# Where a mixture-of-experts kernel issues its loads of gates and activations, and how it splits expert weights

## The chip, the cores and the metric

The kernel runs on one core of one Trainium2 chip. The metric is the device time of one launch in microseconds (us). "Time before" is the median of three launches; the profile is of one further execution.

## The reference

Two transformer blocks over 512 tokens of width 1024, in float32. The first has attention and gated linear attention and then a PEER layer: 128 x 128 = 16384 experts, of which each token picks 16 in each of 8 heads. The second has pooling, spatial gating, a convolutional feed-forward layer and a gate at the end. The change lies in the PEER layer:

```python
q = (xi @ w_q).reshape(n, PEER_HEADS, 2, PEER_KEY_DIM)
...
gate = jax.nn.softmax(best_s, axis=-1)
act = jax.nn.gelu(jnp.einsum('nd,nhkd->nhk', xi, u[idx]), approximate=False)
return jnp.einsum('nhk,nhkd->nd', (gate * act).astype(xi.dtype), v[idx])
```

## The kernel before, in words

**Split operands.** Every large product is made with three matmuls (`mm3`, L86): an operand x is held as a high part (`whi` for weights), which ScalarE (ACT) writes by a rounding copy (L73), and a low part (`wlo`), which VectorE (DVE) writes as x minus the high part (L74). TensorE (PE) adds high times high, high times low and low times high. A weight block comes as one load into `wraw` from SyncE's queue (SP, L58), one block ahead in the program's order; eight `wraw` buffers exist in the expert stages (`c.more` is 5 there and 0 elsewhere). `split` (L64) works in two halves: for each half one tile of `whi` and one of `wlo`, four buffers of each, so two blocks.

**The PEER layer, dense.** For 384 of the 512 tokens all 16384 experts are computed, 128 to a block: an "up" block multiplies the tokens with `u` (24 matmuls of 384 columns) and ACT's Gelu empties the bank (L749); there are two banks. A "down" block multiplies gate times activation (`wh`, `wl`) with `v` into six accumulators (18 matmuls of 512 columns, L1064). The other 128 tokens go by gathered rows: GpSimd (POOL) fetches a row of `u` or `v` (L761), DVE multiplies it (L774) or adds it to an accumulator (L782).

**The two stages.** From about 480 to 965 us come the queries, the routing, and up blocks 0 to 95; the activations go to DRAM as `Ad`, the dense gates as `Gd`. The down stage (`down`, L1000, about 965 to 1640 us) goes through an order written by `down_order`: eight fresh up blocks, whose activations stay on chip (`fresh`), then three runs of eight stored down blocks, then the eight fresh ones as down blocks; and so on. Down blocks are weighed in groups of four: `weigh` (L1025) multiplies activations (`at`) by gates (`gt`) into `wt` on DVE (L1029), ACT copies the high part `wh` (L186), DVE makes the low part `wl` (L187). `gt` covers two groups, `at` one, two buffers each; `wt` has one buffer, `wh` and `wl` two.

**The loads in question.** `load` (L1015) issues `gt` (1.5 MB in runs of 512 bytes, 16 times) and `at` (768 KB, 24 times) from SP's queue, in the program's order eight steps before the group's first block; `weigh` stands two steps before it. `paced` makes a load wait for `c.step`, ACT's latest high-part copy. The gathers of rows are paced in the same way. The order of the instructions in each engine's queue is fixed when the program is built, from a modelled timeline (L1459), so an operation can stand earlier than its line suggests once the model has its inputs ready; on the chip each queue runs in that order.

Of the kernel before, what the change touches and what calls it, by code (L numbers as in the profile page):

```python
# [8 lines left out]
F32 = mybir.dt.float32  # L9
F32R = mybir.dt.float32r  # L10
# [5 lines left out]
ALU = mybir.AluOpType  # L16
# [4 lines left out]
P = 128  # L21
# [26 lines left out]
class Ctx:  # L48
# [15 lines left out]
    def split(self, raw, shape):  # L64

        nc = self.nc
        n = shape[0] // 2
        hi, lo = Halves(n), Halves(n)
        for i in range(2):
            x = raw[:, i * n:(i + 1) * n, :]  # L70
            for h, tag in ((hi, "whi"), (lo, "wlo")):
                h.append(self.wp.tile([P, n, shape[1]], F32R, tag=tag, name=tag, bufs=4))
            self.step = nc.scalar.copy(hi[i], x)  # L73
            nc.vector.tensor_tensor(lo[i], x, hi[i].bitcast(F32), ALU.subtract)  # L74
        return hi, lo

    def weights(self, jobs):
# [107 lines left out]
def split_plain(c, hi, lo, x):  # L185
    c.nc.scalar.copy(hi, x)  # L186
    c.nc.vector.tensor_tensor(lo, x, hi.bitcast(F32), ALU.subtract)  # L187
# [504 lines left out]
DT = ND * P  # L692
GT = 16
NG = DT // GT
JG = 4
JG2 = 2 * JG
NS = 96
KEEP = 1
LOAD = 8
WEIGH = 2  # L700
ROWS = 4
AFTER = 4
# [13 lines left out]
def peer_block(c):  # L716
# [4 lines left out]
    with ExitStack() as ctx:  # L721
# [78 lines left out]
        with ExitStack() as vctx:  # L800
            down(c, vctx, aux, up, bank)
# [198 lines left out]
def down(c, ctx, aux, up, bank):  # L1000
    nc, tc, I, X = c.nc, c.tc, c.I, c.X
    wk = ctx.enter_context(tc.tile_pool(name="pv", bufs=2))
    acc = [aux(f"acc{i}") for i in range(2 * ND)]
    acts, gts, ws = {}, {}, {}
    rate = (2 * P - c.n_rows) / (NKEYS + (NKEYS - NS) - 8)
    due = 0.0

    def turn():
        nonlocal due
        due += rate  # L1010
        while due >= 1:
            next(c.rows, None)
            due -= 1

    def load(j):  # L1015

        j0, b0 = j // JG2 * JG2, j % JG2
        if b0 == 0:
            gts[j0] = wk.tile([P, NG, JG2, GT], F32, name="gt")
            c.paced(nc.sync.dma_start(out=gts[j0], in_=c.Gd[:, :, j0:j0 + JG2, :].rearrange("n i j g -> i n j g")))  # L1020
        if j0 not in acts:
            ws[j] = wk.tile([P, JG, DT], F32, name="at")
            c.paced(nc.sync.dma_start(out=ws[j], in_=c.Ad[j // JG]))  # L1023

    def weigh(j):  # L1025
        j0, b0 = j // JG2 * JG2, j % JG2
        at = acts[j0][:, b0:b0 + JG, :] if j0 in acts else ws[j]
        wt = wk.tile([P, JG, NG, GT], F32, name="wt", bufs=1)
        nc.vector.tensor_tensor(wt, at.rearrange("p j (n g) -> p j n g", g=GT),  # L1029
                                gts[j0][:, :, b0:b0 + JG, :].rearrange("p n j g -> p j n g"), ALU.mult)  # L1030
        w = wt.rearrange("p j n g -> p j (n g)")
        ws[j] = [wk.tile([P, JG, DT], F32R, name=n) for n in ("wh", "wl")]
        split_plain(c, *ws[j], w)

    steps = [(what, j) for what, j0 in c.order for j in range(j0, j0 + JG2)]
    groups = [(s, j) for s, (what, j) in enumerate(steps) if what == "down" and j % JG == 0]
    to_load, to_weigh = list(groups), list(groups)
    n_done, batch = 0, []
    for s, (what, j) in enumerate(steps):
        while to_load and to_load[0][0] - s <= LOAD:  # L1040
            load(to_load.pop(0)[1])
        while to_weigh and to_weigh[0][0] - s <= WEIGH:
            weigh(to_weigh.pop(0)[1])
        if what == "up":
            if j % JG2 == 0:
                acts[j] = c.keep.tile([P, JG2, DT], F32, name="fresh")
            up(j, acts[j // JG2 * JG2][:, j % JG2, :])
            turn()
            continue
        wh, wl = ws[j // JG * JG]  # L1050
        vh, vl = next(c.peer_w)
        batch.append((j % JG, vh, vl))
        n_done += 1
        turn()
        if n_done == NKEYS - 1:
            continue

        last2 = n_done == NKEYS
        for hf in range(2):
            for t in range(ND):  # L1060
                tk = slice(t * P, (t + 1) * P)
                for bi, (jb, bh, bl) in enumerate(batch):
                    for pi, (x, y) in enumerate(((wh, bh), (wh, bl), (wl, bh))):
                        nc.tensor.matmul(acc[2 * t + hf], x[:, jb, tk], y.row(hf), start=n_done == 1 and pi == 0,  # L1064
                                         stop=last2 and bi == len(batch) - 1 and pi == 2)
        batch = []
    for _ in c.rows:
        pass
    for q in range(2):
        for t in (ND, *range(ND)):  # L1070
            if t < ND:
                y = wk.tile([P, 512], F32, tag=("at", "gt")[(q * ND + t) % 2], name="y")
                nc.scalar.copy(y, acc[2 * t + q])
            else:
                y = c.acc3[:, q * 512:(q + 1) * 512]
            o = bank("yt")
            for k in range(4):
                nc.tensor.transpose(o[:, k * P:(k + 1) * P], y[:, k * P:(k + 1) * P], c.ident)
            xs = X[:, 4 * q:4 * q + 4, t * P:(t + 1) * P]
            nc.vector.tensor_tensor(xs, xs, o.rearrange("p (k n) -> p k n", k=4), ALU.add)  # L1080
# [383 lines left out]
```

## Time and profile before

| what | us |
|---|---|
| median of 3 launches | 2466.18 |
| lowest and highest | 2461.13 and 2481.36 |
| the profiled execution, its own time | 2462.88 |
| its span, first to last instruction | 2461.1 |
| PE busy | 2401.9 |
| DVE busy | 1769.1 |
| ACT busy | 1200.6 |

The span is what the profile's rows divide up; 1.8 us of the execution's time lie outside it. PE, PEld, DVE, ACT and POOL are the engines (PEld is PE's loading of stationary operands, which runs beside the matmuls). "Busy" counts an instruction from its start to its end, with overlaps counted once; a matmul's end is modelled. The granted clock is the share of TensorE's full speed that the chip allowed in a stretch: 1.00 is 2.4 GHz, 0.50 is 1.2 GHz.

### The profile page before, as it was taken

What the parts mean: (1) busy time and instruction counts of PE and PEld (TensorE: products, weight loads), DVE (VectorE), ACT (ScalarE), POOL (GpSimd) and SP (SyncE); (2) the same over time, 40 slices, a digit from 0 to 9 for tenths busy, and PEclk for the clock granted to TensorE, in tenths of its full rate; (3) what the DMA queues carried; (4) which work ended last, traced back from release to release, by engine and by line L of the source; (5) the groups of instructions that cost most, each with busy time, mean ns of one, the idle gap of its engine ahead of it and who ended that gap; (6) DMA issues with size and microseconds to landing.
All of it is one profiled execution on the core that took longest, in us unless ns stands there. A gap on an engine that the chain in (4) does not pass through costs nothing.

```text
span 2461.1 us, 34465 instructions
## 1 busy us (share of the span) xinstructions
PE 2401.9 (98%) x12475; PEld 2095.1 (85%) x12475; DVE 1769.1 (72%) x3442; ACT 1200.6 (49%) x2163; POOL 380.6 (15%) x272
## 2 busy tenths in 40 slices
PE   8999899999999999999999999999999999999998
PEld 7888578999999999888878778779888888888888
DVE  5875769999899887786776776766764456777436
ACT  6334654446788995433333333335433335444335
POOL 0000000001333323333343432420000000000000
PEclk9999999999999999999999999999999999999999
DMA  4210034356999999988988888943232332232333
GB/s 138 69 52 27 26 117 143 101 183 209 324 359 349 334 332 359 359 308 287 351 274 301 319 286 307 323 169 100 86 99 95 97 100 96 95 98 97 94 105 103
DMA packets 170296, 471.80 MB, mean 192 GB/s; under 512 B 14060, under 2 KB 66157, under 8 KB 166798
## 3 DMA queue, kind: packets, MB, share of 16 engines
q1 hardware_dynamic: 133262, 335.37, 39.7%
q0 software_dynamic: 36864, 134.23, 15.7%
q8 instruction: 98, 1.61, 0.3%
q14 instruction: 72, 0.59, 0.1%
HBM read 421.31 MB, written 48.23 MB: 191 GB/s over the span
## 4 chain that ended last, share of the span: by engine, by line
PE 64%; DMA 8%; DVE 6%; issue 4%; POOL 1%; ACT 1%; SPq 0%; DVEq 0%; POOLq 0%; ACTq 0%
PE mm L97 51%; PE acc L1064 8%; PE G L946 3%; DMA row<-in_v_t_dram,ev 3%; DMA at<-Ad 2%; DVE wlo L74 2%; DMA wraw<-in_v_t_dram 1%; POOL row L761 1%; DVE acc L782 1%; DMA row<-in_peer_u_dram,eu 1%; PE sc L845 1%; DMA gt<-Gd 1%; DVE eq L898 0%; DVE ij L901 0%; SPq L1023 0%
## 5 line engine op out<-in xcount | busy, mean ns | idle before, releaser
L73 ACT CAST whi<-wraw 128x512 fp32r<-128x512 f32 (+3 forms) x902 | 547.6, 609 | 897.0 <-PE mm L97 524.6
L74 DVE TENSOR_TENSOR wlo<-wraw,whi 128x512 fp32r<-128x512 f32 (+3 forms) x902 | 595.4, 670 | 257.4 <-ACT whi L73 253.9
L97 PE MATMUL mm<-hi,whi 128*128 128x384 f32 (+3 forms) x2016 | 722.5, 363 | 19.8 <-ACT fresh L749 13.7
L97 PE MATMUL mm<-lo,whi 128*128 128x384 f32 (+3 forms) x2016 | 718.4, 361 | 0.5 <-DVE lo L182 0.4
L97 PE MATMUL mm<-hi,wlo 128*128 128x384 f32 (+3 forms) x2016 | 717.6, 361 | 0.3 <-DVE wlo L74 0.3
L97 PEld LDWEIGHTS mm<-hi,whi 128*128 128x128 f32 (+1 forms) x2016 | 377.4, 189 | 58.3 <-ACT fresh L749 14.7
L97 PEld LDWEIGHTS mm<-lo,whi 128*128 128x128 f32 (+1 forms) x2016 | 377.0, 189 | 38.2 <-DVE lo L182 1.7
L97 PEld LDWEIGHTS mm<-hi,wlo 128*128 128x128 f32 (+1 forms) x2016 | 376.9, 189 | 37.9 <-DVE wlo L74 1.9
L1064 PE MATMUL acc<-wlo,wh 128*128 128x512 f32 x768 | 300.8, 392 | 12.3 <-DVE wlo L74 12.3
L1064 PE MATMUL acc<-whi,wl 128*128 128x512 f32 x768 | 299.5, 390 | 0.0
L761 POOL DMA_INDIRECT row<-in_peer_u_dram,eu x128 | 165.8, 1295 | 658.2 <-DMA wraw<-in_u_t_dram 271.5
L761 POOL DMA_INDIRECT row<-in_v_t_dram,ev x128 | 208.3, 1628 | 317.1 <-ACT whi L73 240.0
L1064 PE MATMUL acc<-whi,wh 128*128 128x512 f32 x768 | 245.2, 390 | 0.0
L782 DVE SCALAR_TENSOR_TENSOR acc<-row,act,acc 128x1024 f32<-128x1024 f32 x128 | 163.7, 1279 | 53.0 <-DMA row<-in_v_t_dram,ev 52.9
L1064 PEld LDWEIGHTS acc<-wlo,wh 128*128 128x128 f32 x768 | 144.5, 188 | 47.0 <-DVE wlo L74 17.4
L774 DVE SCALAR_TENSOR_TENSOR row<-row,hn 128x1024 f32<-128x1024 f32 x128 | 155.6, 1218 | 26.1 <-DMA row<-in_peer_u_dram,eu 26.1
L1064 PEld LDWEIGHTS acc<-whi,wh 128*128 128x128 f32 x768 | 144.4, 188 | 30.1
L1064 PEld LDWEIGHTS acc<-whi,wl 128*128 128x128 f32 x768 | 144.6, 188 | 29.7
L943 ACT ACTIVATE oa<-oa,tr 128x128 f32<-128x128 f32 x384 | 122.6, 393 | 22.8 <-DVE oa L941 22.5
L946 PE MATMUL G<-ob,oa 128*128 128x128 f32 x768 | 113.0, 276 | 1.3 <-ACT oa L943 1.3
L946 PEld LDWEIGHTS G<-ob,oa 128*128 128x128 f32 x768 | 108.8, 191 | 2.4 <-ACT oa L943 2.3
L947 ACT COPY gst<-G 128x512 f32<-128x512 f32 x96 | 102.2, 1071 | 15.5 <-PE G L946 14.5
(362 smaller groups left out, 3095.7 us busy)
## 6 DMA issues: line engine op xcount, KB each, us to landing
wraw<-in_u_t_dram SPq DMA_DIRECT2D x128, 512.0 KB, 5.7
wraw<-in_v_t_dram SPq DMA_DIRECT2D x128, 512.0 KB, 7.2
Gd<-gst SPq DMA_DIRECT2D x24, 1024.0 KB, 6.6
gt<-Gd SPq DMA_DIRECT2D x16, 1536.0 KB, 12.1
wraw<-in_w_up_dram SPq DMA_DIRECT2D x44, 512.0 KB, 3.3
Ad<-ast SPq DMA_DIRECT2D x24, 768.0 KB, 5.6
at<-Ad SPq DMA_DIRECT2D x24, 768.0 KB, 11.8
wraw<-in_w_pq_dram SPq DMA_DIRECT2D x16, 512.0 KB, 4.1
```

The lines of the kernel that those rows point to most:

```text
L73: self.step = nc.scalar.copy(hi[i], x)
L74: nc.vector.tensor_tensor(lo[i], x, hi[i].bitcast(F32), ALU.subtract)
L97: nc.tensor.matmul(o, a, b, start=first and ps == 0 and i == 0, stop=last and ps == 2 and i == n - 1)
L761: i = nc.gpsimd.indirect_dma_start(out=t, out_offset=None, in_=table, in_offset=bass.IndirectOffsetOnAxis(ap=idx[:, s:s + 1], axis=0))
L774: nc.vector.scalar_tensor_tensor(u, u, 1.0, hn, op0=ALU.mult, op1=ALU.mult, accum_out=c.act3[:, s:s + 1])
L782: nc.vector.scalar_tensor_tensor(c.acc3, v, c.act3[:, s:s + 1], c.acc3, op0=ALU.mult, op1=ALU.add)
L845: nc.tensor.matmul(o[:, t * P:(t + 1) * P], q[:, t * P:(t + 1) * P], keys[:, f, :], start=True, stop=True)
L943: nc.scalar.mul(oa[:, i, :], oa[:, i, :], tr[:, 2, b0 + i:b0 + i + 1])
L946: nc.tensor.matmul(o[:, i * P:(i + 1) * P], oa[:, i, :], ob[:, i, :], start=True, stop=True)
L947: nc.scalar.copy(st[:, :, b0 - t0:b0 - t0 + TB].rearrange("p j n -> p n j"), o.rearrange("p (n j) -> p n j", n=TB))
L1064: nc.tensor.matmul(acc[2 * t + hf], x[:, jb, tk], y.row(hf), start=n_done == 1 and pi == 0, stop=last2 and bi == len(batch) - 1 and pi == 2)
```

## The change

`load` goes. Two functions, `load_gates` and `load_acts`, issue the same loads from ACT's queue, without pacing. At the start of `down` they are called for the first pair of groups' gates, the first two groups' activations and the second pair's gates; after that each `weigh` calls `load_acts` once (for stored groups) and, in the second group of a pair, `load_gates`, so that a load is issued two groups or two pairs before its use, into the buffer that this `weigh` has just read. In `split` each part of a weight block becomes one tile of the whole block with two buffers, in all stages of the kernel; the high part is still copied in two halves, and in the expert stages the low part is one operation on 128x1024 instead of two on 128x512.

```diff
+        for h, tag in ((hi, "whi"), (lo, "wlo")):
+            whole = self.wp.tile([P, *shape], F32R, tag=tag, name=tag, bufs=2)
+            h += [whole[:, i * n:(i + 1) * n, :] for i in range(2)]
+            h.whole = whole
         for i in range(2):
-            x = raw[:, i * n:(i + 1) * n, :]
-            for h, tag in ((hi, "whi"), (lo, "wlo")):
-                h.append(self.wp.tile([P, n, shape[1]], F32R, tag=tag, name=tag, bufs=4))
-            self.step = nc.scalar.copy(hi[i], x)
-            nc.vector.tensor_tensor(lo[i], x, hi[i].bitcast(F32), ALU.subtract)
+            self.step = nc.scalar.copy(hi[i], raw[:, i * n:(i + 1) * n, :])
+            if not self.more:
+                nc.vector.tensor_tensor(lo[i], raw[:, i * n:(i + 1) * n, :], hi[i].bitcast(F32), ALU.subtract)
+        if self.more:
+            nc.vector.tensor_tensor(lo.whole, raw, hi.whole.bitcast(F32), ALU.subtract)
         return hi, lo
...
-LOAD = 8
...
-    def load(j):
-
-        j0, b0 = j // JG2 * JG2, j % JG2
-        if b0 == 0:
-            gts[j0] = wk.tile([P, NG, JG2, GT], F32, name="gt")
-            c.paced(nc.sync.dma_start(out=gts[j0], in_=c.Gd[:, :, j0:j0 + JG2, :].rearrange("n i j g -> i n j g")))
-        if j0 not in acts:
-            ws[j] = wk.tile([P, JG, DT], F32, name="at")
-            c.paced(nc.sync.dma_start(out=ws[j], in_=c.Ad[j // JG]))
+    def load_gates():
+        j0 = gts_due.pop(0)
+        gts[j0] = wk.tile([P, NG, JG2, GT], F32, name="gt")
+        nc.scalar.dma_start(out=gts[j0], in_=c.Gd[:, :, j0:j0 + JG2, :].rearrange("n i j g -> i n j g"))
+
+    def load_acts():
+        j = ats_due.pop(0)
+        ws[j] = wk.tile([P, JG, DT], F32, name="at")
+        nc.scalar.dma_start(out=ws[j], in_=c.Ad[j // JG])
...
         split_plain(c, *ws[j], w)
 
+        if j < NS and ats_due:
+            load_acts()
+        if b0 and gts_due:
+            load_gates()
+
     steps = [(what, j) for what, j0 in c.order for j in range(j0, j0 + JG2)]
     groups = [(s, j) for s, (what, j) in enumerate(steps) if what == "down" and j % JG == 0]
-    to_load, to_weigh = list(groups), list(groups)
+    to_weigh = list(groups)
+    ats_due, gts_due = [j for _, j in groups if j < NS], [j for _, j in groups if j % JG2 == 0]
+    for f in (load_gates, load_acts, load_acts, load_gates):
+        f()
     n_done, batch = 0, []
     for s, (what, j) in enumerate(steps):
-        while to_load and to_load[0][0] - s <= LOAD:
-            load(to_load.pop(0)[1])
```

## Rows read from the trace of the kernel before

**Rows 1.** The page, part 1: busy time, share, instructions of each engine

```profile
PE 2401.9 (98%) x12475; PEld 2095.1 (85%) x12475; DVE 1769.1 (72%) x3442; ACT 1200.6 (49%) x2163; POOL 380.6 (15%) x272
```

**Rows 2.** Busy time by stage: length, PE, PEld, DVE, ACT, POOL, clock, DMA share, GB/s

```profile
480.00:540.00 60.00, 60.00 (x348) 60.00 (x347) 60.00 (x293) 28.99 (x51) 0.00 (x0) 1.00 0.50 163
540.00:960.00 420.00, 418.64 (x2672) 416.29 (x2671) 377.25 (x686) 330.98 (x729) 124.34 (x99) 1.00 0.88 319
...
1720.00:2461.00 741.00, 731.48 (x3446) 613.58 (x3445) 440.64 (x770) 316.66 (x502) 0.00 (x0) 1.00 0.30 97
```

**Rows 3.** PE by stretch: length, busy (instructions), granted clock, DMA share, GB/s

```profile
980.00:1640.00 660.00, 633.90 (x2905) 0.98 0.89 307
...
1140.00:1150.00 10.00, 4.22 (x15) 0.69 0.47 162
...
1320.00:1330.00 10.00, 9.11 (x43) 0.83 0.67 228
...
1350.00:1360.00 10.00, 6.97 (x29) 0.94 0.98 384
...
1500.00:1510.00 10.00, 10.00 (x44) 0.72 0.78 278
```

**Rows 4.** Waits from 960 to 1660 us: total us, times, longest us

```profile
DVE wt L1029 <- DMA at<-Ad: 57.6, 11, 8.7
DVE acc L782 <- DMA row<-in_v_t_dram,ev: 52.9, 31, 6.4
...
PEld acc L1064 <- DVE wlo L74: 17.4, 13, 3.5
...
PE mm L97 <- ACT fresh L749: 13.7, 3, 5.8
...
PE acc L1064 <- DVE wlo L74: 12.3, 9, 3.0
```

**Rows 5.** Timeline of DVE and of ACT around 1143 us: start, length, instruction, [idle before]

```profile
1142.23 1.76 DVE L1029 TENSOR_TENSOR wt<-at,gt 128x1536 f32<-128x1536 f32 x1 [8.67 <-DMA at<-Ad]
...
1144.03 1.47 ACT L186 CAST wh<-wt 128x1536 fp32r<-128x1536 f32 x1 [9.11 <-DVE wt L1029]
```

**Rows 6.** Timeline of SP's queue of loads: start, length of the issue

```profile
970.10 0.38 SPq L1020 DMA_DIRECT2D gt<-Gd  x1
...
970.53 7.30 SPq L1023 DMA_DIRECT2D at<-Ad  x1
...
978.41 0.55 SPq L1023 DMA_DIRECT2D at<-Ad  x1
...
1126.25 7.79 SPq L1023 DMA_DIRECT2D at<-Ad  x1
```

**Rows 7.** The chain that ended last, pieces in order of time: start, length, what

```profile
476.46 48.38 PE mm L97 x279
...
1231.42 14.03 DMA gt<-Gd
...
1555.39 13.35 DMA at<-Ad
...
1636.25 21.11 PE acc L1064 x93
```

**Rows 8.** The activations' tile at: issues on SP (ns, min/median/max) and landing

```profile
L1023 SPq DMA_DIRECT2D at<-Ad x24: 327/2339/7793, 970.5 to 1573.5; - x24
...
DMA to landing us min/median/max: 4.8/11.8/15.9
```

**Rows 9.** Timeline of ACT in the down stage: whole blocks split in halves

```profile
1271.63 1.13 ACT L73 CAST whi<-wraw 128x512 fp32r<-128x512 f32 x2
...
1292.98 0.62 ACT L73 CAST whi<-wraw 128x512 fp32r<-128x512 f32 x1 [1.42 <-PE acc L1064]
```

**Rows 10.** Groups by shape, 975 to 1645 us: count, busy us, mean ns, idle before

```profile
L74 DVE TENSOR_TENSOR wlo<-wraw,whi 128x512 fp32r<-128x512 f32 x309 | 205.1, 685 | 49.7 <-ACT whi L73 49.7
...
L782 DVE SCALAR_TENSOR_TENSOR acc<-row,act,acc 128x1024 f32<-128x1024 f32 x125 | 159.9, 1279 | 53.0 <-DMA row<-in_v_t_dram,ev 52.9
```

## The prediction

> **What bounds the kernel now.** I read the page first: PE is busy for 2401.9 of 2461.1 us [rows 1], so a change off PE pays only where PE stands idle or slow. The windows by stage say where that is. In the up stage PE is busy for 418.64 of 420 us, and it was for all of 480 to 540, with DVE full as well; in the second block it is 731.48 of 741 [rows 2]. Between 980 and 1640 us, the down stage, it is 633.90 of 660 at a mean clock of 0.98 [rows 3]: 26.1 us idle, all that an edit there can win from idle time. Its floor there is its own matmuls: a down block takes 18 x 21.11/93 = 4.09 us and an up block 24 x 48.38/279 = 4.16 us [rows 7].
>
> Then the waits of that stage. PE lost 13.7 us in three waits for `fresh`, ACT's Gelu, and 12.3 us in nine waits for the low part of a weight block [rows 4]: 26.0, the whole idle time. The Gelu is not slow; it stands behind something. The timeline at 1143 us shows the three links: DVE stood 8.67 us before `wt` until `at` had landed; ACT stood 9.11 us before `wh` until `wt` was made [rows 5]; behind `wh` in ACT's queue lay the Gelu that frees PE's bank. PE was busy for only 4.22 of the 10 us from 1140 [rows 3]. DVE waited 57.6 us in all for `at`, in 11 waits, and 52.9 us for gathered rows, in 31 [rows 4].
>
> Last, why `at` is late. It lands 11.8 us after its issue in the median and 15.9 at most [rows 8]. An issue takes 0.33 us, but right behind a gate load SP is held for 7.30 or 7.79 us [rows 6], and the median over all is 2.34 us [rows 8]. The issue at 1126.25 was wanted by DVE at 1133.6 (1142.23 less 8.67), 7.3 us later, by a queue that had been ordered on the assumption of an earlier landing.
>
> **The change part by part.** The sum is made against the profiled execution, 2462.9 us (2461.1 and 1.8 outside the span), which lies 3.3 us under the median.
>
> *Waits removed.* A load now goes out when the buffer that it fills has just been read, two groups before its use. A group is four down blocks, 16.4 us, and `wh` has two buffers, so one weighing follows another at about that pace; the lead becomes at least 16.4 us and mostly 30, against a longest landing of 15.9 [rows 8]. So the waits for `at` and `gt` should go. What they cost PE: 13.7 us through the Gelu; 3.0 us in the window at 1350, where `at` was awaited; and about 4 us in four waits of some 1 us for low parts that the chain traces to a `gt` or `at` (1231 and 1555 us are the first and last of them) [rows 3, 4, 7]. Together 20.7 us. At least the 13.7 go, at most all 26.1: the stage's next late thing is the gathered row, and part of the wait for `at` may only turn into a wait for a row.
>
> *Clock regained.* The granted clock is below 1.00 only after these stalls: 0.69, 0.83, 0.94 and 0.72 in the four stretches shown [rows 3]. At 1320 that is 9.1 x 0.17 = 1.5 us of full-speed work, at 1500 it is 2.8, at 1140 1.3, at 1350 0.4: 6 us, between 0 and 6.
>
> *The first four loads.* At the entry to the down stage SP needed 0.38 for `gt`, 7.30 for the `at` behind it and 0.55 for the next [rows 6]; with a second gate load that is 8.6 us, now in ACT's queue, in front of high parts and Gelus of the fresh up blocks. No row shows a load on ACT, but one shows ACT held there for 9.11 us by something else [rows 5], and PE lost 5.8 us to it [rows 3, 4]. I take 6 us and 1 us of clock: +7. It is 0 if the loads happen to fall where ACT idles, 8.6 and 2 of clock if nothing covers it.
>
> *The other 36 issues.* At 0.33 to 0.38 us each they hold ACT for 13 us over the stage. They are issued when `wt` has been read, which the `wh` beside them waits for anyway, so they add no wait. ACT mostly waits for PE there: 1.42 us ahead of each half's copy [rows 9]. Taken at 0; 0.35 us once in 16.4 us would cost 13 us only if ACT had no idle time. SP loses 40 issues and their pacing; weight loads no longer queue behind a gate load, but they run eight buffers ahead, so again 0, and a gain of at most the 1 us that one low part lost that way.
>
> *The low part in one operation.* Two of 128x512 take 685 ns each; 128x1024 of a like operation takes 1279 [rows 10]: 0.09 us of DVE saved per block, 13 us over the 144 expert blocks, and none of it on PE's path, which pays where DVE and PE are both full, from 480 to 540 [rows 2]: 0, at best -1.
>
> *The whole-block tile.* This is the cost. Before, a half's copy starts when PE has let go of that half: 0.62 us of copy and 0.69 of low part against three half blocks, 6.1 us, until PE wants it: 4.8 us spare. Afterwards both copies wait for the end of the block: 1.13 us for two [rows 9] and 1.28 for the low part [rows 10] against one block, 4.09: 1.7 us spare, for everything that stands before it in two queues. In the down stage the loading of operands already met a late low part 13 times [rows 4]; each of these ends about 0.6 us later, when the second half's share is done too: +8. The least is 0; at most each of the 31 row waits passes on 0.6 us, 19. In the up stage DVE is 90% and ACT 79% busy [rows 2] and PE hardly waits; there I take 0 and allow 10. In the other stages the low parts stay halves and blocks are longer; 0, at most 4.
>
> Sum: -20.7 - 6 + 7 + 8 = -11.7, so 2462.9 - 11.7 = 2451 us. What is late next is the gathered row.
>
> **The rivals.** *All gain, no price* (0.22): the loads on ACT fall into its idle time and the 1.7 us suffice. -20.7 - 6 and some of the other 5 us of idle time, about -28: 2435. For it: ACT is 49% busy overall [rows 1]. Against it: 13 late low parts already.
>
> *The one-piece low part starves PE* (0.14): it decides wherever the queues of ACT and DVE together delay a low part by over 1.7 us block after block, as rows that land late and a DVE that is 90% full can do. Then the whole-block tile costs its bounds, 19 and 10 us, and the gain from the waits falls to the 13.7 and the clock: 2462.9 - 13.7 - 6 + 7 + 19 + 10 = 2479.
>
> *ACT takes over SP's hold* (0.08), the slower case: in the second group of a pair `load_acts` stands before `load_gates`, but both become free at the same instant. If they are queued the other way round, twelve times an `at` follows a gate load on ACT and holds it for some 5.5 us (7.30 and 7.79 are rows that show it [rows 6]). A hold of 9.11 cost PE 5.8, so 3.3 us were covered; the smaller spare time takes that to about 2. 12 x 3.5 = 42 us, and 6 of clock that is not regained: 2451 + 42 + 6, about 2499. In the order as written the next `at` comes 16 us later and finds the hold over. The Trainium skill (Perfetto Trace Analysis, the section DMA Instruction — HWDGE) says that the block that generates descriptors is shared between the sequencers that issue such loads and locked by one at a time; by that rule the hold also reaches across queues, from a weight load on SP to an `at` on ACT, which no row here can show, with one queue in use.
>
> *The loads land no sooner* (0.05): with the 16 DMA engines at a share of 0.89 [rows 3], an earlier issue could simply meet other traffic, and DVE would wait as before. The costs alone remain: 2462.9 + 7 + 8 = 2478. The Trainium skill (DMA: Bandwidth & Descriptors, Issuing engines are not separate DMA queues) has a rule that speaks for this: the same 16 engines carry what every queue issues, so another queue only saves the sequencer's time, usually small. Here that time is not small, 7.30 us behind a gate load [rows 6], and the change also moves the issue ahead by a group; by the rule the time would be the 2478.
>
> **How the numbers follow.** The forecast has 0.51. A measurement of this kernel can tell about 1% from no change, 25 us (its three runs span 20). Faster by over 1% means under 2441.5: most of the first rival and the lower edge of the forecast, 0.23. Slower by over 1% means over 2490.8: most of the third and a tail of the second, 0.09. The rest, 0.68, is within 1%. The range runs from 2434, the clean gain, to 2480, which takes in the forecast with its costs at their bounds (19 for the tile, 10.6 for the first loads: 2466) and the two rivals at 2478 and 2479.
>
> **What would show it.** The waits of the down stage: `wt` for `at` near 0 instead of 57.6 us, no wait for `fresh` but one shortly after 970 us, where ACT issues the first four loads; waits of PE for low parts as many or more than nine, each traced to a gathered row or to ACT's copies; the clock at 1.00 but for the entry. In the up stage PE stays over 99% busy. I am wrong if `at` issues on ACT last several us all through the stage, if `wt` still waits for `at`, or if PE begins to wait for low parts in the up stage.

## The result, and the profile after the change

The changed kernel is slower: 2481.48 us in the median of 16 runs (2474.61 to 2492.40) against 2468.89 for the kernel before in 16 (2458.59 to 2481.36). The ratio is 1.0056, with a 95% interval from 1.0042 to 1.0069: 13 to 14 us more, where 12 fewer had been forecast. The profiled execution took 2474.61 us, 11.7 more than that of before, with a span of 2472.6; the forecast of 2451 had been made on such an execution.

The page's first part (busy time, share, instructions) answers to [rows 1]. PE has 6.5 us more busy time for the same 12475 matmuls; DVE has 272 fewer instructions and 27 us less work.

```profile
PE 2408.4 (97%) x12475; PEld 2094.8 (85%) x12475; DVE 1741.8 (70%) x3170; ACT 1158.2 (47%) x2163; POOL 357.2 (14%) x272
```

The windows of the stages, with the columns of [rows 2]: the up stage, in which PE had 1.4 us of idle time, has 9.0 now.

```profile
480.00:540.00 60.00, 58.86 (x336) 57.19 (x334) 60.00 (x299) 29.26 (x50) 0.00 (x0) 1.00 0.46 153
540.00:960.00 420.00, 412.13 (x2614) 408.57 (x2614) 365.14 (x596) 326.46 (x720) 123.27 (x93) 1.00 0.85 306
1720.00:2461.00 741.00, 740.61 (x3530) 623.57 (x3529) 431.75 (x763) 297.60 (x501) 0.00 (x0) 1.00 0.31 97
```

The last window holds other work than in [rows 2], since it starts at another point of the program; the length of what follows the down stage is compared below. PE alone, in stretches of the down stage (length, busy, granted clock, DMA share, GB/s), beside [rows 3]:

```profile
980.00:1640.00 660.00, 641.86 (x2957) 0.99 0.90 315
990.00:1000.00 10.00, 5.94 (x27) 0.80 1.02 307
1370.00:1380.00 10.00, 7.47 (x27) 0.83 0.66 198
1440.00:1450.00 10.00, 7.92 (x35) 1.00 0.75 221
```

The down stage has 8 us less idle time than before (18.1 against 26.1); one loss is at its entry, the others lie behind 1370 us. The waits between 990 and 1650 us (total, times, longest), beside [rows 4]:

```profile
PE acc L1073 <- DVE wlo L78: 10.5, 9, 2.5
PE mm L101 <- ACT fresh L752: 3.3, 1, 3.3
...
PE mm L101 <- DVE wlo L78: 2.6, 2, 1.9
...
DVE acc L785 <- DMA row<-in_v_t_dram,ev: 61.1, 38, 5.1
```

`wt` waits for no operand any more, and PE for `fresh` once. Nine waits for a late low part of a down block are there as before, though the late `at` is not, and two of a fresh up block have joined them. In the up stage new waits stand on PE:

```profile
PE mm L101 <- DVE wlo L78: 2.9, 4, 1.1
PE mm L101 <- ACT ast L752: 5.0, 5, 1.9
```

To compare whole stages, three times are enough, shown here for after: first and last start of the up blocks' Gelu (`ast`), and the last start of a matmul of the down stage.

```profile
L752 ACT ACTIVATE ast<-mm x96: 467/484/524, 483.1 to 981.8; 128x384 f32<-128x384 f32 x96
...
L1073 PE MATMUL acc<-whi,wl x768: 387/389/628, 1022.7 to 1670.4; 128*128 128x512 f32 x192
```

Differences of such times give the table, for every run (us): until the first `ast`; up to the last `ast` (the up stage); from there to the last matmul of `acc` (the down stage); the rest of the span.

| kernel | start | up | down | rest | span |
|---|---|---|---|---|---|
| before | 479.0 | 485.7 | 692.9 | 803.5 | 2461.1 |
| after | 483.1 | 498.7 | 688.6 | 802.2 | 2472.6 |
| e1, loads alone | 480.0 | 486.8 | 662.7 | 802.3 | 2431.8 |
| e2, split alone | 486.6 | 498.5 | 697.2 | 802.8 | 2485.1 |
| e3, whole tile, two low parts | 482.6 | 491.9 | 681.6 | 803.0 | 2459.1 |
| e4, loads alone, from SP | 480.4 | 487.0 | 660.3 | 802.6 | 2430.3 |
| e5, after with a third whole tile | 487.5 | 487.0 | 657.3 | 804.0 | 2435.8 |
| e5c, e1 with six raw buffers | 478.4 | 486.1 | 667.4 | 802.3 | 2434.2 |
| e6, pacing taken away alone | 479.7 | 487.9 | 659.5 | 803.5 | 2430.6 |
| e7, e1 without gathered rows | 480.1 | 486.5 | 655.3 | 802.5 | 2424.4 |
| e8, after without gathered rows | 482.5 | 506.1 | 661.0 | 803.6 | 2453.2 |
| e9, e4 with a third block of halves | 480.0 | 488.3 | 654.9 | 802.2 | 2425.4 |
| e10, e4 with pacing | 478.9 | 486.5 | 659.9 | 803.6 | 2428.9 |

Of the 11.5 us that the span grew, the up stage has 13.0 and the start 4.1; the down stage gave back only 4.3.

PE between the same times (length, busy, granted clock, DMA share, GB/s): up and down stage of before, up and down stage of after, down stage of e1.

```profile
479.00:964.70 485.70, 484.34 (x3051) 1.00 0.83 300
964.70:1657.60 692.90, 666.80 (x3070) 0.99 0.87 301
```

```profile
483.10:981.80 498.70, 489.69 (x3053) 1.00 0.81 291
981.80:1670.40 688.60, 669.36 (x3070) 0.99 0.87 303
```

```profile
966.80:1629.50 662.70, 658.78 (x3071) 0.99 0.89 314
```

Idle time is not the whole loss. Of the 13.0 us in the up stage 7.6 are idle time; for the other 5.4 PE is busy longer with as many matmuls. Of the 25.9 us between e1 and after in the down stage 15.3 are idle time and 10.6 longer busy time. The waits listed here explain the idle part; the longer busy time was not traced.

**How a late low part comes about, in the down stage of after.** Three timelines between 1366 and 1376 us (start, length, instruction, [idle before]): DVE's, then ACT's, then PE's.

```profile
1370.68 1.28 DVE L785 SCALAR_TENSOR_TENSOR acc<-row,act,acc 128x1024 f32<-128x1024 f32 x1 [3.51 <-DMA row<-in_v_t_dram,ev]
1371.88 1.75 DVE L191 TENSOR_TENSOR wl<-wt,wh 128x1536 fp32r<-128x1536 f32 x1
1373.55 1.22 DVE L78 TENSOR_TENSOR wlo<-wraw,whi 128x1024 fp32r<-128x1024 f32 x1
```

```profile
1368.06 1.13 ACT L74 CAST whi<-wraw 128x512 fp32r<-128x512 f32 x2
1370.98 1.14 ACT L74 CAST whi<-wraw 128x512 fp32r<-128x512 f32 x2 [1.79 <-PE acc L1073]
```

```profile
1374.83 0.80 PE L1073 MATMUL acc<-wlo,wh 128*128 128x512 f32 x1 [2.52 <-DVE wlo L78]
```

The high part of the block was there at 1368.06 + 1.13 = 1369.19, and with 1.22 us for the low part all could have been ready at 1370.4. PE wanted it at 1374.83 - 2.52 = 1372.31: 1.9 us spare, as the prediction had worked out (1.7). But DVE stood until 1370.68 for a gathered row, and the accumulation and a `wl` of 1.75 us lay in front. The low part ended 4.4 us late; PE lost 2.52 us, and the granted clock was 0.83 in that stretch.

The other eight waits look alike: in each, DVE ended a wait for a row 2 to 5 us before PE's late matmul started, and worked without a gap from there to the low part. The rows also say where the losses fall. PE's busy time from 1020 to 1370 us, then DVE's waits for rows, first in that stretch and then from 1370 to 1660:

```profile
1020.00:1370.00 350.00, 349.94 (x1631) 1.00 0.93 333
```

```profile
DVE acc L785 <- DMA row<-in_v_t_dram,ev: 2.4, 5, 0.9
```

```profile
DVE acc L785 <- DMA row<-in_v_t_dram,ev: 56.9, 32, 5.1
```

While the rows came in time, PE lost nothing to the whole-block tiles; all nine waits lie where the rows came late. Why they come late from 1370 us on was not traced.

**In the up stage it is ACT's queue.** ACT and PE around 592 us:

```profile
592.15 1.14 ACT L74 CAST whi<-wraw 128x512 fp32r<-128x512 f32 x2 [4.07 <-PE mm L101]
593.19 0.48 ACT L752 ACTIVATE ast<-mm 128x384 f32<-128x384 f32 x1
```

```profile
593.73 0.44 PE L101 MATMUL mm<-hi,whi 128*128 128x384 f32 x1 [1.44 <-ACT ast L752]
```

Both copies wait for PE's end of a whole block, 4.07 us, and behind them in the queue stands the Gelu that frees PE's bank; PE waits 1.44 us for that Gelu. ACT's waits for PE ahead of a copy between 470 and 990 us, before and after:

```profile
ACT whi L73 <- PE mm L97: 94.2, 83, 1.7
```

```profile
ACT whi L74 <- PE mm L101: 91.0, 44, 4.2
```

With halves the longest was 1.7 us; now it is 4.2. Before, PE did not wait for `ast` at all in that stretch. The 5.0 us for `ast`, the 2.9 for low parts and 1.0 for another tile of ACT's make up the 9.0 us of idle time.

### The profile page after: what moved, and what is told of

Same layout as the page of the kernel before. It is cut to its first block, busy times and chain, and to the rows that moved or that the text cites. A ratio compares the mean times of both kernels' runs of the same rounds, so it can differ in the third digit from the quotient of the medians.

```text
span 2472.6 us, 33685 instructions
## 1 busy us (share of the span) xinstructions
PE 2408.4 (97%) x12475; PEld 2094.8 (85%) x12475; DVE 1741.8 (70%) x3170; ACT 1158.2 (47%) x2163; POOL 357.2 (14%) x272
## 4 chain that ended last, share of the span: by engine, by line
PE 76%; issue 8%; DVE 7%; DMA 5%; POOL 2%; ACT 2%; ACTq 0%; POOLq 0%; DVEq 0%; SPq 0%
PE mm L101 53%; PE acc L1073 15%; DMA row<-in_v_t_dram,ev 3%; PE G L949 2%; POOL row L764 2%; DVE wlo L78 1%; PE mm L534 1%; DMA row<-in_peer_u_dram,eu 1%; PE da L635 1%; DMA wraw<-in_u_t_dram 1%; PE mm L608 1%; PE sc L848 1%; ACT whi L74 0%; PE e L101 0%; ACT pe L612 0%
## 5 line engine op out<-in xcount | busy, mean ns | idle before, releaser
L74 ACT CAST whi<-wraw 128x512 fp32r<-128x512 f32 (+3 forms) x902 | 503.2, 606 | 850.9 <-PE mm L101 407.9
L78 DVE TENSOR_TENSOR wlo<-wraw,whi 128x1024 fp32r<-128x1024 f32 x272 | 331.8, 1220 | 108.5 <-ACT whi L74 99.3
L76 DVE TENSOR_TENSOR wlo<-wraw,whi 128x512 fp32r<-128x512 f32 (+2 forms) x358 | 219.3, 647 | 101.6 <-ACT whi L74 101.4
L764 POOL DMA_INDIRECT row<-in_v_t_dram,ev x128 | 180.4, 1410 | 366.6 <-ACT whi L74 217.4
L1073 PE MATMUL acc<-whi,wh 128*128 128x512 f32 x768 | 195.0, 389 | 0.0
L946 ACT ACTIVATE oa<-oa,tr 128x128 f32<-128x128 f32 x384 | 122.2, 393 | 11.2 <-DVE oa L944 10.4
L949 PE MATMUL G<-ob,oa 128*128 128x128 f32 x768 | 107.4, 277 | 1.1 <-ACT oa L946 1.0
## 6 DMA issues: line engine op xcount, KB each, us to landing
gt<-Gd ACTq DMA_DIRECT2D x16, 1536.0 KB, 22.5
```

The costliest lines, as they stand in the source:

```text
L74: self.step = nc.scalar.copy(hi[i], raw[:, i * n:(i + 1) * n, :])
L76: nc.vector.tensor_tensor(lo[i], raw[:, i * n:(i + 1) * n, :], hi[i].bitcast(F32), ALU.subtract)
L78: nc.vector.tensor_tensor(lo.whole, raw, hi.whole.bitcast(F32), ALU.subtract)
L764: i = nc.gpsimd.indirect_dma_start(out=t, out_offset=None, in_=table, in_offset=bass.IndirectOffsetOnAxis(ap=idx[:, s:s + 1], axis=0))
L946: nc.scalar.mul(oa[:, i, :], oa[:, i, :], tr[:, 2, b0 + i:b0 + i + 1])
L949: nc.tensor.matmul(o[:, i * P:(i + 1) * P], oa[:, i, :], ob[:, i, :], start=True, stop=True)
```

## The experiments

The theory after this reading: the split costs what the loads gain. With two buffers of a whole block instead of four of a half, the next block's copies start a half block later, and the spare time that is left, under 2 us, is shorter than the delays that stand in DVE's and ACT's queues anyway (some expectations call this theory D). Rivals: the loads gain less than they should, since they lie on ACT's queue, in front of its copies and Gelus; the loads bring back the cost elsewhere; the late low parts come from the rows alone, whatever the split. In the ratios, each kernel stands against runs of the kernel before on the same chip. Each diff is against the kernel that its heading starts from: e1 and e6 against before, e2, e3, e5 and e8 against after, e4 and e7 against e1, e9 and e10 against e4; "..." marks what is left out.

**e1: the loads alone**, as the change has them, with the split of before.

```diff
-            c.paced(nc.sync.dma_start(out=ws[j], in_=c.Ad[j // JG]))
+        nc.scalar.dma_start(out=ws[j], in_=c.Ad[j // JG])
...
+        if j < NS and ats_due:
+            load_acts()
+        if b0 and gts_due:
+            load_gates()
```

> Only the loads of gates and activations are moved to ACT's queue; weight blocks are split as before. Theory A (the whole-block tile is what costs, the loads pay): the waits of the down stage for at and gt go, the entry loses about 7 us, and the time falls by about 15 us, ratio 0.994 (0.990 to 0.997). Rival B (the loads on ACT's queue cost what was lost, the split is free): as slow as the whole change, ratio 1.004 to 1.008. Rival C (it is the one operation for the low part, not the tile): the same as A here.

Measured: 2435.02 us (2431.37 to 2438.64), ratio 0.9867 [0.9840, 0.9894]. The loads alone win 33 us, more than twice what was expected; the down stage is 30.2 us shorter and the other stages stay within 1.2. PE's waits between 960 and 1660 us, where 26.0 us stood in [rows 4]:

```profile
PE acc L1069 <- ACT whi L73: 3.3, 1, 3.3
...
PE acc L1069 <- DVE wlo L74: 0.6, 2, 0.4
```

Not only the Gelu's waits went, but nearly all of the nine for low parts too, with rows still late on DVE (38.7 us in 28 waits).

**e2: the split alone**, with the loads of before.

```diff
+LOAD = 8
...
-        nc.scalar.dma_start(out=ws[j], in_=c.Ad[j // JG])
+            c.paced(nc.sync.dma_start(out=ws[j], in_=c.Ad[j // JG]))
```

> Only the split is changed (whole-block tiles, two buffers, one low-part operation in the expert stages); the loads are SP's as before. Theory A: the up stage, the stage before it and the down stage lose as in the whole change, and nothing is gained back: 17 us before the down stage and 8 or more in it, ratio 1.010 (1.007 to 1.014). Rival B: ratio 0.998 to 1.001. Rival C: the same as A here.

Measured: 2484.62 us (2477.76 to 2490.78), ratio 1.0064 [1.0041, 1.0088]. PE's waits between 480 and 1690 us:

```profile
PE acc L1068 <- DVE wlo L78: 18.1, 16, 2.3
PE mm L101 <- DVE wlo L78: 13.2, 13, 2.1
PE mm L101 <- ACT ast L753: 5.0, 5, 1.9
```

So PE waits 31.3 us for low parts in place of 12.3, and the up stage is 12.8 us longer, without any edit of the loads. The waits for `fresh`, 13.7 us before, are gone here, though the loads are the old ones and DVE still waits 30.3 us for `at`: in the down stage PE's waits come to 29.1 us, where 26.0 stood. The ratio is below the 1.007 that was the least expected. Split and loads do not add: 16 us of cost alone, yet 46 on top of e1. In the down stage the split costs 4.3 us beside the old loads (697.2 against 692.9) and 25.9 beside the new ones (688.6 against 662.7): where PE stood still because of `at` anyway, late weight blocks could catch up, or the one wait took the place of the other (argued from the waits, not shown). Beside the new split the new loads win 3 us, within the intervals, where beside the old one they win 33.

**e3: the whole-block tile, with two low parts** of a half each.

```diff
-            if not self.more:
-                nc.vector.tensor_tensor(lo[i], raw[:, i * n:(i + 1) * n, :], hi[i].bitcast(F32), ALU.subtract)
-        if self.more:
-            nc.vector.tensor_tensor(lo.whole, raw, hi.whole.bitcast(F32), ALU.subtract)
+            nc.vector.tensor_tensor(lo[i], raw[:, i * n:(i + 1) * n, :], hi[i].bitcast(F32), ALU.subtract)
```

> The whole change, but the low part of a weight block is again two operations on halves in the expert stages too, into the same whole-block tiles with two buffers. Theory A (the tile's release is the cost): most of the loss stays, up stage 10 us or more longer than before, ratio 1.002 to 1.007. Rival C (the one operation is the cost): the up stage is back at its 486 us, only the 4 us of the first stage stay lost, and the loads' gain shows: ratio 0.994 to 0.998. Rival B: no difference from the whole change, 1.005.

Measured: 2452.49 us (2446.07 to 2461.89), ratio 0.9940 [0.9916, 0.9963]. By the medians the tile costs 17 us over e1 and the single operation 29 more; by the times of the profiled executions it is 27 and 14, but e3's is its slowest but one of seven and that of after the fastest of its sixteen, so these make the operation's share look small. Both parts cost, where each of the two expectations had named one; which costs more is not settled. By stages (after less e3) the single operation costs 6.8 us in the up stage and 7.0 in the down stage, although it takes 1220 ns where two halves take 2 x 685 [rows 10]. The page's group of it in after (count, busy us, mean ns, idle before):

```profile
L78 DVE TENSOR_TENSOR wlo<-wraw,whi 128x1024 fp32r<-128x1024 f32 x272 | 331.8, 1220 | 108.5 <-ACT whi L74 99.3
```

The Trainium skill (VectorE: DVE Perf Modes, Rules for kernel authors) advises, for DVE operations that follow one another, to minimize their number. Here DVE's own work agrees with it, 27 us less of it, and the kernel's time does not: the one operation starts when the second half's copy is done, and PE gets the first half of the low part no sooner than the second.

**e4: the loads of e1, from SP's queue**, at the same places and not paced.

```diff
-        nc.scalar.dma_start(out=ws[j], in_=c.Ad[j // JG])
+        nc.sync.dma_start(out=ws[j], in_=c.Ad[j // JG])
```

> As the run with the loads alone, but the same loads are issued from SP's queue at the same places, two groups ahead and not paced; split as before. If the earlier issue is what pays and ACT's entry stall costs 7 us: ratio 0.991, 2 to 7 us below the run from ACT's queue. If it is the queue that pays (a load on SP waits for a buffer to be read and holds back the weight loads behind it): 0.997 to 1.003, with PE waiting for weight loads.

Measured: 2430.92 us (2425.12 to 2432.02), ratio 0.9842 [0.9819, 0.9864]. SP does as well as ACT or 4 us better: the intervals overlap, and the down stage is 2.4 us shorter. It is not the queue that pays. The Trainium skill (DMA: Bandwidth & Descriptors, Issuing engines are not separate DMA queues) has it that all queues feed the same 16 engines and that another issuer saves only issue time; e4 beside e1 agrees.

**e5: the whole change with a third whole-block buffer** in the expert stages; its room comes from two of the eight raw buffers.

```diff
-RAW, MORE = 3, 5
+RAW, MORE = 3, 3
...
+        self.n_w = (self.n_w + 1) % 3
...
-            whole = self.wp.tile([P, *shape], F32R, tag=tag, name=tag, bufs=2)
+            third = self.more and self.n_w == 2
+            whole = (self.rp if third else self.wp).tile([P, *shape], F32R, tag=tag, name=tag, bufs=1 if third else 2)
```

> The whole change, but in the expert stages the whole-block tiles of both parts rotate over three buffers instead of two; the room comes from the raw weight buffers, six there instead of eight. Theory D (the whole-block tile leaves a low part too little spare time; the loads are sound): with a block more of spare time the up stage is back at 486 to 489 us and the down stage at about 660, only the 3 to 4 us of the first stage stay lost: ratio 0.988 (0.985 to 0.992). Rival E (it is not spare time: the one long operation, or the order of the queues that comes with it, costs whatever the buffers): ratio 1.000 to 1.006.

Measured: 2436.76 us (2435.19 to 2446.67), ratio 0.9886 [0.9862, 0.9910]. Tile and operation are those of after; with a block more between release and use the up stage is back at 487.0 us and the down stage at 657.3. PE's and DVE's waits, 990 to 1650 us:

```profile
PE mm L104 <- ACT fresh L755: 2.1, 1, 2.1
...
PE acc L1076 <- DVE wlo L81: 0.2, 1, 0.2
```

```profile
DVE acc L788 <- DMA row<-in_v_t_dram,ev: 48.5, 27, 5.6
```

DVE still stands for rows, up to 5.6 us at a time, and PE no longer notices.

**e5c: the control for e5**, e1 with six raw buffers (`RAW, MORE = 3, 3`).

> Control for the run with three buffers: the loads alone from ACT's queue, split as before, but six raw weight buffers in the expert stages instead of eight. Both theories: like the loads alone, ratio 0.985 to 0.990; if the weight loads need the eight buffers, 0.990 to 0.997, and the run with three buffers is to be read against this one.

Measured: 2432.88 us (2429.39 to 2436.00), ratio 0.9857 [0.9836, 0.9877], as e1. The two raw buffers are not missed, and their loss is no part of e5's gain.

**e7: e1 without the gathered rows** of the down stage, and **e8: after without them**. The output then lacks what these rows add.

```diff
     def turn():
-        nonlocal due
-        due += rate
-        while due >= 1:
-            next(c.rows, None)
-            due -= 1
+        pass
...
-    for _ in c.rows:
-        pass
```

> The loads alone from ACT's queue, split as before; all gathered rows of the down stage are left out, with the DVE operations on them (the rows' part of the result for 128 tokens stays incomplete). The down stage is already within 3 us of PE's own 657 with the rows, so little can be won: ratio 0.983 to 0.988.

> The whole change, with the gathered rows of the down stage left out in the same way. Theory D, with the rows as what eats the spare time: the down stage falls from 685 to 657 to 662 us, and only the loss of the two stages before it (17 us) stays: ratio 0.990 to 0.995. Rival F (the chain of copies, low part and block end alone is too long, rows or not): the down stage stays above 675 us, ratio 0.998 to 1.004.

Measured: e7 2426.01 us (2424.66 to 2426.51), ratio 0.9832 [0.9812, 0.9851]; e8 2454.49 (2447.17 to 2459.42), ratio 0.9940 [0.9920, 0.9961]. Without rows the down stage of after falls from 688.6 to 661.0 us, that of e1 only from 662.7 to 655.3: of the 25.9 us between the two, 20 go with the rows. PE's waits for low parts between 990 and 1650 us are down to one of 0.8 us. With the rows go DVE's work on them and their share of the DMA traffic (share 0.58 in place of 0.87), so that e8 does not say which of the two a row costs by; the timelines of after speak for DVE's queue. The up stage of e8, whose code is that of after, came out longer (506.1 against 498.7), with 8.0 us of PE's waits for ACT's `oa`, a small tile of the dense gates, in place of 1.0; the queues' order is planned anew for each program, and which difference of order did it was not traced. So e8's total says less than its down stage.

**e6: the kernel before, its two loads not paced**, and nothing else changed; **e10: e4 with pacing**, so that only the place is new; **e9: e4 with three blocks' worth of half buffers**, as an attempt at a better version.

```diff
-            c.paced(nc.sync.dma_start(out=ws[j], in_=c.Ad[j // JG]))
+            nc.sync.dma_start(out=ws[j], in_=c.Ad[j // JG])
```

```diff
-        nc.sync.dma_start(out=ws[j], in_=c.Ad[j // JG])
+        c.paced(nc.sync.dma_start(out=ws[j], in_=c.Ad[j // JG]))
```

```diff
-RAW, MORE = 3, 5
+RAW, MORE = 3, 3
...
+        self.n_w = (self.n_w + 1) % 3
+        third = self.more and self.n_w == 2
...
-                h.append(self.wp.tile([P, n, shape[1]], F32R, tag=tag, name=tag, bufs=4))
+                h.append((self.rp if third else self.wp).tile([P, n, shape[1]], F32R, tag=tag, name=tag, bufs=2 if third else 4))
```

> The kernel before, except that its loads of gates and activations on SP's queue are no longer paced by ACT's latest copy; they stand where they stood, eight steps before use. If the pacing is what made them late: the down stage falls to 657 to 662 us, ratio 0.984 to 0.988, as with the loads moved on SP's queue. If the place in the program decides: ratio 0.996 to 1.002, and DVE still waits tens of us for at.

> The loads from SP's queue at their new places, two groups ahead, but paced by ACT's latest copy as before; split in halves. If the place decides: like the unpaced loads from there, ratio 0.984 to 0.988. If the pacing is what made the loads late: 0.994 to 1.000.

> The loads from SP's queue, two groups ahead and not paced, with the split in halves as before, and in the expert stages three blocks' worth of half buffers instead of two (six raw buffers instead of eight). PE's matmuls of the down stage need about 651 us and the best run took 657 there: with a third block of spare time 652 to 655, ratio 0.980 to 0.984. If spare time no longer limits anything: as the loads from SP's queue alone, 0.984.

Measured: e6 2432.40 us (2425.99 to 2432.59), ratio 0.9846 [0.9821, 0.9870]; e10 2434.44 (2431.02 to 2436.77), ratio 0.9869 [0.9842, 0.9896]; e9 2427.13 (2424.36 to 2428.15), ratio 0.9835 [0.9813, 0.9858]. To take `paced` off two lines of the kernel before wins as much as the change's whole rebuilding of the loads. The issue then goes out when the buffer is free. Two timelines of e6, DVE's and SP's:

```profile
1102.62 1.75 DVE L1029 TENSOR_TENSOR wt<-at,gt 128x1536 f32<-128x1536 f32 x1
```

```profile
1104.40 0.33 SPq L1023 DMA_DIRECT2D at<-Ad  x1
```

`wt` ends reading `at` at 1104.37, and the next `at` is issued 0.03 us later, 31 us before the `wt` that reads it (1135.62, the third weighing of this run of stored blocks). For the first weighing of the run, at 1102.62, `at` was issued at 1039.12; in the kernel before, the same load was issued at 1126.25 [rows 6], 7.3 us before DVE wanted it. But e10 shows that the pacing does no harm at the new place. Old place and pacing together made the loads late, and to change either is enough. How they did is not shown: in the kernel before, the issues of these loads waited only 15.1 us in all for a copy of ACT's (9.2 for `gt`, 5.9 for `at`), at most 2.9 at a time, and in e10 such waits are longer (49.1 us in all) and cost nothing. Their place in SP's queue, which is planned with the pacing, is the likelier cause. What was expected of e10 for the case that pacing alone is to blame did not come. e9 beats both kernels and has the lowest time of all that compute the whole output (e7's 2426.01 lacks the rows), but its interval overlaps those of e4 and e6: with halves and timely loads there is little left for a third buffer to win.

## Why the prediction was wrong

The prediction gave 2451 us, with a range of 2434 to 2480; 2481.48 lies 1.5 us above it and on the other side of the kernel before. Its sum was -11.7 against the profiled execution; measured against such an execution it is +11.7. By its steps:

- **Waits removed (-20.7), clock (-6), first four loads (+7), other issues (0).** Right in kind, too small in size. Together -19.7; measured in e1 -29.3 by the spans, 33 by the medians. Of the low-part waits, 12.3 us in nine, I let 7 us in five end with the loads (the one of 3.0 and four of some 1 us), and took the rest for the rows'. In e1 0.6 us are left, with rows still late: so nearly all nine hung on the late loads, for which DVE had waited 57.6 us (`at`) and 11.2 (`gt`). With the 13.7 for `fresh` that is 25.4 in place of 20.7. The rest of the difference: one wait of 3.3 us for a long issue in place of 6, and 8.0 us less busy time of PE for as many matmuls (666.80 to 658.78) in place of 6 less 1 of clock. PE's idle time fell, in 600 us from 1000 on, from 25.4 (574.64 busy) to 3.5 (596.48).
- **The first four loads** came as described. ACT's timeline at the entry:

```profile
989.26 0.40 ACTq L1021 DMA_DIRECT2D gt<-Gd  x1
989.70 6.13 ACTq L1026 DMA_DIRECT2D at<-Ad  x2
995.87 0.45 ACTq L1021 DMA_DIRECT2D gt<-Gd  x1
996.37 0.49 ACT L752 ACTIVATE fresh<-mm 128x384 f32<-128x384 f32 x1 [6.70 <-issue]
```

  7.06 us on ACT; PE lost 4.06 of the 10 us from 990 and ran at 0.80 in the rest and at 0.86 in the next 10, 1.2 and 1.4 more: 6.7 against +7. In e1 these four cost nothing, but the fifth load, one of the other 36 taken at 0, held ACT for 9.95 us from 992.17: 3.3 us of PE's time, and 2.4 of clock in the 10 us from 1000 (0.66). In e4, where SP issues them, ACT's Gelus of the fresh blocks stand without such a gap.
- **The low part in one operation (0, at best -1).** Wrong in sign: 14 us by the spans, 29 by the medians (after against e3). I priced DVE's time and not when the result is there. That price was too small too, without harm to the sum: 272 blocks are split this way and not 144, and DVE has 27 us less work, not 13.
- **The whole-block tile (+8; 0 in the up stage, 0 elsewhere).** This is the step that failed, together with the one before it: both together were put at +8 or 7, and measured 40.8 us over e1 by the spans, of them 3.1 before the up stage, 11.9 in it, 25.9 in the down stage (46 us by the medians). The 1.7 us of spare time was right, 1.9 in the case shown. What failed is what I held against it: I counted the 13 low parts that were late already, and gave each 0.6 us. The right measure was the length of the delays that 4.8 us of spare time had covered until then: waits for rows of up to 5.1 us and, behind them, `wl` and `wt` of 1.75 us each. And I took PE's lack of waits in the up stage for spare time, where DVE is full until 540 us and a Gelu stands behind ACT's copies.
- **Rival 2, the one-piece low part, priced 2479 at 0.14,** is what happened: its condition (queues delay a low part by over 1.7 us, block after block) holds, and its costs of 19 and 10 us came out as 25.9 and 11.9. It expected the gain of the loads to fall to the 13.7 and the clock; the loads gained more and the split cost more, so that its time is near for two errors that cancel. Rival 1 would have needed the spare time to suffice; rival 4 is excluded, since the loads land in time.
- **Rival 3, ACT held by issues,** did not decide. `at` issues take 0.338 us in the median, and ACT stood for a few long ones. The issues of after (ns, min/median/max) and the landing, beside [rows 8]:

```profile
L1026 ACTq DMA_DIRECT2D at<-Ad x24: 326/338/5651, 989.7 to 1553.4; - x24
...
DMA to landing us min/median/max: 4.3/7.1/14.3
```

- **What would show it.** `wt` for `at` near 0, one wait for `fresh` near the entry, nine low-part waits, each behind a wait for a row: all seen. A clock of 1.00 but for the entry: not quite (0.83 in the ten us from 1370, 1460, 1510 and 1640, after PE had stood). PE over 99% busy in the up stage: it has 98.1% (470.99 of 480), and PE waits for low parts there, which the text had named as the mark of being wrong.

That spare time is the cause is shown from three sides: taken away alone (e2), it makes PE wait; given back with the change otherwise whole (e5), the cost is gone but for the start; with the rows left out (e8), 20 of the 25.9 us in the down stage go. One thing no run holds fixed: the queues' order is planned anew for each kernel, so that a few us in each of these differences can be the order's. Open stay the exact split between tile and operation, the 2 to 9 us in the first stages (start at 482.5 to 487.5 us in all kernels with whole tiles, 478.4 to 480.4 in all with halves), where PE's wait for a small tile of DVE's, `pe`, grew from 2.1 us to 6.0, and the order that made e8's up stage longer.

## What to carry to other kernels

A tile's size sets when its buffer is released: before halves are merged, work out the spare time from release to use, and hold it against the longest delay that stands in the queues of the engines that fill it, not against the delays that show; a bottleneck engine that never waits says nothing of how near it is to waiting. Time each part of a combined change alone, and add nothing up: the split cost 16 us beside the old loads and 46 beside the new. When a load comes late, look first at what it is made to wait for and where it stands in the program; to remove the pacing was worth as much as another queue.

## What the runs showed of the hardware

Gate loads (1.5 MB in runs of 512 bytes) land later from ACT's queue than from SP's: 22.6 us after the issue in the median in e1 (17.1 to 29.4) and 22.5 in after, against 16.2 in e4 from SP at the same places, 15.6 in e6 and 12.1 in the kernel before, where they were paced. Why was not tried. And an `at` can be held long after a gate load: not only right behind it, as in [rows 6], but with 10 us of other work between. ACT's queue in after:

```profile
1019.73 0.38 ACTq L1021 DMA_DIRECT2D gt<-Gd  x1
1030.68 5.47 ACTq L1026 DMA_DIRECT2D at<-Ad  x1
```

The issue began 11 us after the gate load and ended 16.4 us after it. In e1 one of 9.95 us began 12.3 us after a gate load at 979.87 and ended 22.2 after it. The prediction had taken the hold to be past when the next `at` comes 16 us after a gate load. In after the `at` issues that come 13 to 16 us after one take 0.33 to 2.86 us and end at most 16.7 us after it, so that it was nearly so; in e1 two ended 19.2 and 22.2 us after theirs. Whether SP's weight loads take part in that hold was not tried.
